# Seven products for eight in the w1/w3 pairs of the 512-token FFNs of a diffusion backbone in split fp32, with two weight sums added up by DMA, another memory layout and another place for the background adaLN work

## Chip, cores and metric

One NeuronCore of a Trainium2 chip runs the whole program in one launch. The metric is device time in microseconds (us), the median of several executions. The program is bound to one core, so nothing is exchanged with others.

## What is computed

Two layers over 512 tokens (256 latent tokens, 256 context tokens), D_MODEL 1024, D_FF 2816, all in float32. Each layer: half an FFN, a token mixer of three branches, half an FFN; each with an adaLN shift, scale and gate (nine vectors "mods" a layer, from `c @ w_ada`). The second layer's last FFN needs the 256 latent tokens only.

```python
def swiglu(h, w1, w3, w2):
    return (jax.nn.silu(h @ w1) * (h @ w3)) @ w2

x = x + 0.5 * m[:, 2] * swiglu(modulate(rms_norm(x, norm_g[l, 0]), m[:, 0], m[:, 1]),
                               ffn_w1[l, 0], ffn_w3[l, 0], ffn_w2[l, 0])
xc = xc + 0.5 * mc[2] * swiglu(modulate(rms_norm(xc, norm_g[l, 0]), mc[0], mc[1]),
                               ffn_w1[l, 0], ffn_w3[l, 0], ffn_w2[l, 0])
```

`x` are the latent tokens, `xc` the context tokens; both go through the same weights.

## The kernel before, in words

The stages are f00 (FFN), mixer 0, f01, f10 (FFNs of 512 tokens), mixer 1, f11 (FFN of 256 tokens) and the output. Activations lie channels on partitions, tokens along the row; a matmul multiplies a 128x128 block of weights with 512 (or 256) tokens.

fp32 accuracy comes from splitting each operand in a high and a low part of type fp32r: every block product is three matmuls, hi by hi, hi by lo and lo by hi (`mm3`, L280 to L282). Inputs are split once. Weights are split as they come: SP loads a tile of 512 KB (4 row blocks x 256 columns, `load_raw`) into one of four places `wr`, ScalarE (ACT) casts it to `whi` (L285), VectorE (DVE; for some tiles GpSimd, POOL) takes the difference as `wlo` (L286). Four pairs of places `wh` hold split weights, so the cast of the fifth waits for the last matmul of the first.

An FFN has 11 column pairs g; pair g is 256 columns of w1 (into PSUM tile p1) and the same 256 of w3 (p3). Each is 8 row blocks (two weight tiles) x 2 column blocks x 3 = 48 matmuls of 512 tokens, 96 for the pair (`product`). Then Silu (L607, ACT), the product with p3 (L608, DVE) and the split in `ghi` and `glo`. Pairs 0 to 5 are the first half, 6 to 10 the second; after each half `to_residual` multiplies with the rows of w2 that belong to it: four column groups of 256 columns, in chunks of up to four row blocks, and adds the result to the residual stream (`xT`, L507, four of 128x256 for each column group). In the second half the squares of the residual are summed for the next norm (`sq` on ACT, `acc_f` on DVE, L312), and the fourth column group is worked together with the next stage's first products (`handover`).

The adaLN vectors of later stages are computed beside the FFNs (`ada`, L200 to L224): a mod is eight steps, each loading 512 KB of w_ada and doing two passes of 128x1024 on DVE (`aacc`, L208, L210), and a ninth with a few small matmuls. `tick()` issues them evenly over the 56 products of an FFN: six mods in f00, five in f01, five in f10, none in mixers and f11.

The order of the instructions on each engine is made by a scheduler at build time; the engines then work through it in order and wait on semaphores. In the built program the hidden inputs `hhi`, `hlo` start at 43 and 59 KiB of each partition, the split weights lie from 91 to 123 KiB, `ghi` starts at 132 and `glo` at 156 KiB.

## Time and profile before

| | |
|---|---|
| median of 3 runs | 2013.01 us (2012.78 to 2013.74) |
| the profiled execution | 2012.76 us, its span 2011.0 us |
| mean granted clock of TensorE | 0.996 |
| busy | TensorE 1981.5 us, VectorE 1330.9, ScalarE 836.3, GpSimd 51.7 |
| matmuls | 11087 |
| read from HBM | 283.50 MB, 143 GB/s over the span |

The profile is of one execution. Busy times say what an engine did, the waits what it stood for, and the chain which work set the end. Matmuls overlap, so the distance from one start to the next, not the length of one, is what a matmul costs. The stages of the FFN f10 in the trace: first w1/w3 half to 1319.4 us, first w2 half to 1388.2, second w1/w3 half to 1500.5, second w2 half to 1547.

### The profile page before, as it was taken

The numbers are of one execution on the slowest core, as the hardware profiler recorded it, in microseconds if no ns is written. First come the engines' busy times: TensorE is split into PE (matmuls) and PEld (weight loads), VectorE is DVE, ScalarE is ACT, GpSimd is POOL, SyncE is SP. The second block draws the span as 40 slices with busy tenths as digits, with TensorE's granted clock in tenths as the row PEclk, the third lists the DMA queues.
The fourth block names the chain that finished last, engine by engine and source line by source line (L and its number), as shares of the span: only waits on it lengthen the run. The fifth ranks groups of instructions, "written<-read, shape, count | busy, mean of one in ns | idle before, by whom it ended". The sixth has DMA issues, their size and how long they took to land.

```text
span 2011.0 us, 27970 instructions
## 1 busy us (share of the span) xinstructions
PE 1981.5 (99%) x11087; PEld 1685.1 (84%) x11087; DVE 1330.9 (66%) x2038; ACT 836.3 (42%) x1286; POOL 51.7 (3%) x32
## 2 busy tenths in 40 slices
...
PEclk8999999999999999999999999999999999999999
...
GB/s 298 217 178 173 172 172 173 115 97 83 77 53 97 118 89 123 120 160 146 176 168 157 134 69 189 178 156 125 166 168 105 64 88 143 145 196 162 187 185 115
DMA packets 240507, 288.47 MB, mean 143 GB/s; under 512 B 14368, under 2 KB 222328, under 8 KB 240120
## 3 DMA queue, kind: packets, MB, share of 16 engines
q1 hardware_dynamic: 240376, 286.69, 46.3%
...
HBM read 283.50 MB, written 3.15 MB: 143 GB/s over the span
## 4 chain that ended last, share of the span: by engine, by line
PE 92%; DVE 3%; ACT 2%; DMA 2%; issue 1%; POOL 0%; SPq 0%; DVEq 0%; ACTq 0%; POOLq 0%
PE p L280 14%; PE p L281 14%; PE p L282 14%; PE py L280 8%; PE py L281 8%; PE py L282 8%; PE pg L282 3%; PE pg L281 3%; PE pg L280 3%; PE pj L281 2%; PE pj L280 2%; PE pj L282 2%; PE pv L809 1%; PE pv L810 1%; PE pv L811 1%; DMA wada<-w_ada 1%
## 5 line engine op out<-in xcount | busy, mean ns | idle before, releaser
L285 ACT CAST whi<-wraw 128x1024 fp32r<-128x1024 f32 (+2 forms) x408 | 406.4, 1000 | 943.6 <-PE p L281 417.0
L286 DVE TENSOR_TENSOR wlo<-wraw,whi 128x1024 fp32r<-128x1024 f32 (+2 forms) x380 | 445.0, 1177 | 348.4 <-ACT whi L285 347.4
L280 PE MATMUL p<-hhi_f,whi 128*128 128x512 f32 (+1 forms) x1440 | 516.1, 359 | 0.4 <-DVE hhi_f L352 0.4
L282 PE MATMUL p<-hhi_f,wlo 128*128 128x512 f32 (+1 forms) x1440 | 513.3, 356 | 1.1 <-POOL wlo L286 0.6
L281 PE MATMUL p<-hlo_f,whi 128*128 128x512 f32 (+1 forms) x1440 | 513.9, 357 | 0.2
L280 PEld LDWEIGHTS p<-hhi_f,whi 128*128 128x128 f32 x1440 | 272.3, 189 | 48.3 <-ACT whi L285 5.9
L282 PEld LDWEIGHTS p<-hhi_f,wlo 128*128 128x128 f32 x1440 | 272.3, 189 | 41.1 <-POOL wlo L286 1.3
L210 DVE SCALAR_TENSOR_TENSOR aacc<-wada,cs,aacc 128x1024 f32<-128x1024 f32 x224 | 277.3, 1279 | 42.6 <-DMA wada<-w_ada 42.3
L281 PEld LDWEIGHTS p<-hlo_f,whi 128*128 128x128 f32 x1440 | 272.3, 189 | 38.8 <-DVE hlo_f L357 1.0
L280 PE MATMUL py<-ghi,whi 128*128 128x512 f32 (+1 forms) x764 | 269.0, 352 | 0.0
L281 PE MATMUL py<-glo,whi 128*128 128x512 f32 (+1 forms) x764 | 267.6, 350 | 0.0
L282 PE MATMUL py<-ghi,wlo 128*128 128x512 f32 (+1 forms) x764 | 267.5, 350 | 0.0
L280 PEld LDWEIGHTS py<-ghi,whi 128*128 128x128 f32 x764 | 143.9, 188 | 26.1 <-issue 4.2
L282 PEld LDWEIGHTS py<-ghi,wlo 128*128 128x128 f32 x764 | 143.9, 188 | 21.3
L281 PEld LDWEIGHTS py<-glo,whi 128*128 128x128 f32 x764 | 143.9, 188 | 21.0
L280 PE MATMUL pg<-hhi_m,whi 128*128 128x512 f32 (+1 forms) x384 | 132.5, 345 | 0.0
L282 PE MATMUL pg<-hhi_m,wlo 128*128 128x512 f32 (+1 forms) x384 | 130.6, 340 | 1.3 <-DVE wlo L286 1.2
L281 PE MATMUL pg<-hlo_m,whi 128*128 128x512 f32 (+1 forms) x384 | 130.3, 339 | 0.0
L286 POOL TENSOR_TENSOR wlo<-wraw,whi 128x768 fp32r<-128x768 f32 (+2 forms) x28 | 51.5, 1842 | 1732.0 <-ACT whi L285 1675.0
L507 DVE SCALAR_TENSOR_TENSOR xT<-py,gmod,xT 128x256 f32<-128x256 f32 x136 | 59.1, 478 | 54.5 <-PE py L282 54.2
L280 PE MATMUL pj<-hhi_m,whi 128*128 128x256 f32 (+1 forms) x288 | 92.9, 323 | 0.0
L281 PE MATMUL pj<-hlo_m,whi 128*128 128x256 f32 (+1 forms) x288 | 92.7, 322 | 0.2
...
## 6 DMA issues: line engine op xcount, KB each, us to landing
wraw<-ffn_w SPq DMA_DIRECT2D x256, 512.0 KB, 3.8
wada<-w_ada SPq DMA_DIRECT2D x128, 512.0 KB, 3.8
wraw<-w_in SPq DMA_DIRECT2D x64, 512.0 KB, 3.6
...
wraw<-w_out SPq DMA_DIRECT2D x16, 512.0 KB, 3.4
...
```

The costliest lines, as they stand in the source:

```text
L210: v.scalar_tensor_tensor(acc[:, t], w, cs[:, k, t:t + 1], acc[:, t], op0=ALU.mult, op1=ALU.add)
L280: te.matmul(o, a, xh, start=start, stop=False)
L281: te.matmul(o, a, xl, start=False, stop=False)
L282: te.matmul(o, b, xh, start=False, stop=stop)
L285: s.copy(hi, src)
L286: eng.tensor_tensor(lo, src, hi.bitcast(F32), ALU.subtract)
L507: v.scalar_tensor_tensor(X[0][:, d, c], acc, gate[:, d, t:t + 1], X[0][:, d, c], op0=ALU.mult, op1=ALU.add)
L809: te.matmul(o, hhi[:, kk, ts], hi[:, k], start=(kk == 0), stop=False)
L810: te.matmul(o, hhi[:, kk, ts], lo[:, k], start=False, stop=False)
L811: te.matmul(o, hlo[:, kk, ts], hi[:, k], start=False, stop=(kk == KD - 1))
```

## The change

*Seven products.* For g = 3 to 10 in f00, f01 and f10 (24 pairs) the pair's work is seen as a product of a 2x2 matrix of weight blocks (w1 or w3; rows 0 to 511 or 512 to 1023) with a 2x2 matrix of input blocks (the same row halves; latent or context tokens), and done with seven block products in place of eight (`seven`, L636 to L683). In what follows P1 to P7 are these products in the order of the text: with w1's first row half (P1, bank b), w3's two halves added (P2, bank c), that sum and w1's first half (P3, b), w1's second half (P4, a tile of its own), w1's first and w3's first half (P5, b), a sum of four (P6, c), w3's second half (P7, b). Each is 4 row blocks x 2 column blocks x 3 = 24 matmuls (L655) of 256 tokens, 168 in all. Banks b and c are the two halves of one PSUM tile, and bank b goes on accumulating from P1 through P3 and P5 to P7. Between them what has been summed so far is read out: copies on ACT of q1 (L660, after P1), p5 (L663, after P2) and w1 (L667, after P3), additions on DVE (L670 after P4, L672 after P5, L676 after P6). In the built program each of P2, P3, P5, P6 and P7 waits for the readout before it, on whichever half of the tile that is. Two Silu (L679, L680) and two passes of DVE (L681, L683) make the gated result.

*Weight sums.* Of the four sums of weight tiles two are made by DMA: the first tile is loaded by SP, and GpSimd then issues a DMA that adds the second from HBM to it (L646, two a group, 48 in all). The other two are passes of DVE over 128x1024 (L665, L674), which the scheduler puts one group ahead of their use. A group splits seven tiles (before: four) and loads five by SP. `wr` has five places.

*Input forms.* `Forms` (L594) makes four sums of input blocks once an FFN, at g = 1 and 2: some twelve DVE passes of 128x1024 and the splits.

*Layout.* Split weights, `ghi` and `glo` of the 512-token FFNs lie below 128 KiB (from 42, 58, 74 and 98 KiB); hidden inputs and the input forms above (`hhi` 175, `hlo` 191, `zone0` 151, `zone1` 163). In f11 `ghi` and `glo` take the two zones.

*Background steps.* f00, f01 and f10 have four mods each, mixer 0 three (27 steps), f11 one. In the three FFNs five steps come at g = 2, the other 31 in the w2 stages, 1.55 for each chunk.

The diff, cut to what is spoken of:

```diff
--- before.py
+++ after.py
-    xp = ctx.enter_context(tc.tile_pool(name="xp", bufs=1))
-    hp = ctx.enter_context(tc.tile_pool(name="hp", bufs=1))
-    wr = ctx.enter_context(tc.tile_pool(name="wr", bufs=4))
+    sm = ctx.enter_context(tc.tile_pool(name="sm", bufs=2))
+    wr = ctx.enter_context(tc.tile_pool(name="wr", bufs=5))
     wh = ctx.enter_context(tc.tile_pool(name="wh", bufs=4))
-    sm = ctx.enter_context(tc.tile_pool(name="sm", bufs=2))
+
+    ctx.enter_context(tc.tile_pool(name="pad", bufs=1)).tile([P, 8], F32, name="pad")
+    xp = ctx.enter_context(tc.tile_pool(name="xp", bufs=1, side="right"))
+    hp = ctx.enter_context(tc.tile_pool(name="hp", bufs=1, side="right"))
+    tz = ctx.enter_context(tc.tile_pool(name="tz", bufs=1, side="right"))
+    sp = ctx.enter_context(tc.tile_pool(name="sp", bufs=1, side="right"))
+    hp.tile([P, 16], F32, name="pad")
...
+    def zone(i, dt=F32):
+        return tz.tile([P, 3 * D], dt, tag=f"t{i}", name=f"zone{i}")
+
+    def half_zone(i, dt=F32):
+        return sp.tile([P, 3 * NTOK], dt, tag=f"v{i}", name=f"half{i}")
+
+    def weight_places(n):
+
+        z = [zone(i, F32R).rearrange("p (a k n) -> p a k n", a=3, k=4) for i in range(2)]
+        if n == 2:
+            return [(z[0][:, 0], z[0][:, 1]), (z[1][:, 0], z[1][:, 1])]
+        return [(z[0][:, i], z[1][:, i]) for i in range(n)]
...
+    class Forms:
+
+
+        def __init__(self, norm, fp):
...
+            whole(t[0], h11, l11)
+            whole(t[1], h12, l12)
+            whole(t[2], h22, l22)
+            v.tensor_tensor(t[0], t[0], t[1], ALU.subtract)
+            v.tensor_tensor(t[1], t[2], t[1], ALU.subtract)
+            split_act(z[0][:, 0], z[1][:, 0], t[0])
+            split_act(z[0][:, 2], z[1][:, 2], t[1])
+            v.scalar_tensor_tensor(t[0], t[0], -1.0, t[2], op0=ALU.mult, op1=ALU.subtract)
+            whole(t[1], h21, l21)
+            split_act(z[0][:, 1], z[1][:, 1], t[0])
+            v.scalar_tensor_tensor(t[0], t[0], -1.0, t[1], op0=ALU.mult, op1=ALU.subtract)
+            self.fourth = lambda: split_act(h12, l12, t[0])
+            self.b11, self.b21, self.b22, self.t4 = (h11, l11), (h21, l21), (h22, l22), (h12, l12)
+            self.t1, self.t2, self.t3 = ((z[0][:, i], z[1][:, i]) for i in range(3))
...
+    def seven(fm, wa, wb, c0, gt):
+
+        q1, p5, w1 = fm.places()
+        pab, pc = psum("p1"), psum_bg("p3")
+        b, c, a = pab[:, 0], pab[:, 1], pc[:, 0]
+
+        def raw(w, i, *more):
+
+            t = load_raw([rowsof(w, 4 * i, 4, c0, 2 * P)], 4, 2 * P)
+            for w, i in more:
+                gp.dma_start(t, rowsof(w, 4 * i, 4, c0, 2 * P), accum_op=ALU.add)
+            return t
+
+        def part(o, w, x, first=False):
+            whi, wlo = split(w, 4, 2 * P)
+            for k in range(4):
+                for m in range(2):
+                    om, cm = o[:, m * L:(m + 1) * L], slice(m * P, (m + 1) * P)
+                    for n, (wt, xt) in enumerate(((whi, x[0]), (whi, x[1]), (wlo, x[0]))):
+                        te.matmul(om, wt[:, k, cm], xt[:, k], start=(first and k == m == n == 0),
+                                  stop=(k == 3 and m == 1 and n == 2), skip_group_check=True)
+
+        a11 = raw(wa, 0)
+        part(b, a11, fm.b11, True)
+        s.copy(q1, b)
+        s1 = raw(wb, 0, (wb, 1))
+        part(c, s1, fm.t1, True)
+        s.copy(p5, c)
+        s2 = fm.sum_place()
+        v.tensor_tensor(s2, s1, a11, ALU.add)
+        part(b, s2, fm.t2)
+        s.copy(w1, b)
+        a12 = raw(wa, 1)
+        part(a, a12, fm.b21, True)
+        v.tensor_tensor(q1, a, q1, ALU.add)
+        part(b, raw(wa, 0, (wb, 0)), fm.t3)
+        v.tensor_tensor(p5, b, p5, ALU.add)
+        s4 = fm.sum_place()
+        v.tensor_tensor(s4, s2, a12, ALU.add)
+        part(c, s4, fm.b22)
+        v.tensor_tensor(w1, c, w1, ALU.add)
+        g1, g2 = gt[:, :, 0:L], gt[:, :, L:]
+        q1, p5, w1, b3 = (x.rearrange("p (m n) -> p m n", m=2) for x in (q1, p5, w1, b))
+        s.activation(g1, q1, AF.Silu)
+        s.activation(g2, w1, AF.Silu)
+        v.scalar_tensor_tensor(g2, p5, -1.0, g2, op0=ALU.mult, op1=ALU.mult)
+        part(b, raw(wb, 1), fm.t4)
+        v.scalar_tensor_tensor(g1, b3, -1.0, g1, op0=ALU.mult, op1=ALU.mult)
...
+            rates = (1.25, (len(mods) * (KD + 1) - 5) / 20) if both else (0.8, 0.0)
+
+            def tick(rate):
+                due[0] += rate
+                n = int(due[0] + 1e-6)
+                due[0] -= n
                 with norm.done():
-                    background(want - state[1])
-                state[1] = max(want, state[1])
+                    background(n)
...
+                    if both and g > 2:
+                        seven(fm, w1, w3, g * 2 * P, gt)
+                        split_act(ghi[:, j, 0:nt], glo[:, j, 0:nt], gt)
+                        continue
...
+                            if g == 2 or not both:
+                                tick(rates[0])
...
+                    if both and g == 1:
+                        with norm.done():
+                            fm = Forms(norm, fp)
+                    if both and g == 2:
+                        fm.fourth()
+                for _ in to_residual(w2, nk, (ghi, glo), nt, gmod[l][:, f], st if half else None, fp, weights, 2 * g0,
                                      then):
-                    tick()
+                    tick(rates[1])
...
+            pending[:] = [ada(*m, mp) for m in mods]
+
+            def tick(n=1):
+                with entry.done():
+                    background(n)
...
+                    tick()
...
+                for n, _ in enumerate(merged(2, psum_bg, mm)):
+                    tick(n % 4 > 0)
...
+                for n, _ in enumerate(to_residual(I["w_out"][l], KD, (mhi, mlo), nq, gmod[l][:, 2], st, mm, weight_places,
+                                                  entry=then)):
+                    tick(2)
...
-    ffn(0, 0, NTOK, after, [(0, m) for m in range(2, 8)], entry)
+    ffn(0, 0, NTOK, after, [(0, m) for m in range(2, 6)], entry)
-    mixer(0, NTOK, entry, after)
+    mixer(0, NTOK, entry, [(0, m) for m in (6, 7, 8)], after)
-    ffn(0, 1, NTOK, after, [(0, 8)] + [(1, m) for m in range(4)], entry)
+    ffn(0, 1, NTOK, after, [(1, m) for m in range(4)], entry)
-    ffn(1, 0, NTOK, entry, [(1, m) for m in range(4, 9)], after)
+    ffn(1, 0, NTOK, entry, [(1, m) for m in range(4, 8)], after)
-    mixer(1, L, after, entry)
-    ffn(1, 1, L, entry, [], Output())
+    mixer(1, L, after, [], entry)
+    ffn(1, 1, L, entry, [(1, 8)], Output())
...
+    nc = _bacc.Bacc("TRN2", target_bir_lowering=False, num_devices=1, dynamic_dma_scratch_size=2048)
```

The order on ScalarE, at two groups of w1/w3. Before, in f10 (`whi` from `wraw` is a weight's cast, `gt` the Silu, L285 CAST `ghi` the split of the gated result):

```order
L285 CAST ghi<-gt 128x1024
L285 CAST whi<-wraw 128x1024 x2
L607 ACTIVATE gt<-p_9672 128x1024
L285 CAST whi<-wraw 128x1024 x2
L285 CAST ghi<-gt 128x1024
L285 CAST whi<-wraw 128x1024 x2
L607 ACTIVATE gt<-p_9811 128x1024
```

With the change, in f01, from the cast for P6 of one group to the cast for P5 of the next; the casts for P7, P1', P2', P3' and P4' (an apostrophe: the next group) are whi_9810, whi_9846, whi_9878, whi_9908 and whi_9939:

```order
L663 COPY half1_8017<-p1_9617 128x512
L306 CAST whi_9810<-wraw_9808 128x1024
L667 COPY w1_8018<-p1_9617 128x512
L306 CAST whi_9846<-wraw_9844 128x1024
L679 ACTIVATE gt_9616<-half0_8016 128x2x256
L306 CAST whi_9878<-wraw_9875 128x1024
L306 CAST whi_9908<-half1_8017 128x1024
L680 ACTIVATE gt_9616<-w1_8018 128x2x256
L306 CAST whi_9939<-wraw_9937 128x1024
L306 CAST ghi_9164<-gt_9616 128x1024
L660 COPY half0_8016<-p1_9842 128x512
L306 CAST whi_9971<-wraw_9968 128x1024
```

Where two casts stood between a Silu and a `ghi`, three copies out of PSUM now stand among seven casts; the cast for P7 comes ahead of the copy that P5 waits for, the cast for P4' and `ghi` ahead of the one that P2' waits for.

The order on TensorE, where one product ends and the next begins. Before, between w3 of one pair and w1 of the next (f10):

```order
L280 MATMUL p3_9961<-hhi_f10_9055,whi_10038 128x512
L281 MATMUL p3_9961<-hlo_f10_9056,whi_10038 128x512
L282 MATMUL p3_9961<-hhi_f10_9055,wlo_10039 128x512
L280 MATMUL p1_10099<-hhi_f10_9055,whi_10103 128x512
L281 MATMUL p1_10099<-hlo_f10_9056,whi_10103 128x512
L282 MATMUL p1_10099<-hhi_f10_9055,wlo_10104 128x512
```

With the change, in f01, behind P7: the last three of the eight matmuls of P1' that follow it, the first four of P4' (p3_9843), and the first of P2' (zone0, zone1 hold the input forms):

```order
L655 MATMUL p1_9842<-hhi_f01_7264,whi_9846 128x256
L655 MATMUL p1_9842<-hlo_f01_7265,whi_9846 128x256
L655 MATMUL p1_9842<-hhi_f01_7264,wlo_9847 128x256
L655 MATMUL p3_9843<-hhi_f01_7264,whi_9939 128x256
L655 MATMUL p3_9843<-hlo_f01_7265,whi_9939 128x256
L655 MATMUL p3_9843<-hhi_f01_7264,wlo_9940 128x256
L655 MATMUL p3_9843<-hhi_f01_7264,whi_9939 128x256
L655 MATMUL p1_9842<-zone0_7846,whi_9878 128x256
L655 MATMUL p1_9842<-zone1_7847,whi_9878 128x256
```

A product no longer runs from end to end. The whole order of a steady group is: 8 of P1', 4 of P4', all of P2', 13 of P4', all of P3', the last 7 of P4', all of P5', 8 of the next P1, all of P6', 8, all of P7', and the last 8.

The order on VectorE in the second w2 half, where the first and the second of its column groups end. Before, in f01:

```order
L507 SCALAR_TENSOR_TENSOR xT<-py,gmod_118,xT 128x256 x3
L217 COPY mrow<-pa_3_8823 128x512
L312 TENSOR_TENSOR acc_f_6865<-acc_f_6865,sq 128x256
L507 SCALAR_TENSOR_TENSOR xT<-py,gmod_118,xT 128x256
L220 TENSOR_TENSOR modT_114<-pa_3_8823,biasT_115 128x16
L286 TENSOR_TENSOR wlo<-wraw,whi 128x1024
L312 TENSOR_TENSOR acc_f_6865<-acc_f_6865,sq 128x256
L286 TENSOR_TENSOR wlo<-wraw,whi 128x1024 x3
L286 TENSOR_TENSOR wlo<-wraw,whi 128x512 x2
L507 SCALAR_TENSOR_TENSOR xT<-py,gmod_118,xT 128x256 x3
```

With the change, from the end of the first column group's residual; the `xT` of the second stand at L528 behind the eight `aacc`, and the `wlo` behind them is the third column group's first weight:

```order
L528 SCALAR_TENSOR_TENSOR xT<-py,gmod_124,xT 128x256
L233 SCALAR_TENSOR_TENSOR aacc<-wada,cs,aacc 128x1024
L333 TENSOR_TENSOR acc_f_7708<-acc_f_7708,sq 128x256
L233 SCALAR_TENSOR_TENSOR aacc<-wada,cs,aacc 128x1024 x7
L528 SCALAR_TENSOR_TENSOR xT<-py,gmod_124,xT 128x256 x3
L333 TENSOR_TENSOR acc_f_7708<-acc_f_7708,sq 128x256
L528 SCALAR_TENSOR_TENSOR xT<-py,gmod_124,xT 128x256
L333 TENSOR_TENSOR acc_f_7708<-acc_f_7708,sq 128x256
L307 TENSOR_TENSOR wlo<-wraw,whi 128x1024
L333 TENSOR_TENSOR acc_f_7708<-acc_f_7708,sq 128x256
L233 SCALAR_TENSOR_TENSOR aacc<-wada,cs,aacc 128x1024
L333 TENSOR_TENSOR acc_f_7708<-acc_f_7708,sq 128x256
```

Before, weights stood in a row ahead of the second column group's residual; now the background passes stand there, and the weight comes behind.

## Rows read from the trace of the kernel before

**Rows 1.** The page, part 1: busy us, share of the span, instructions, by engine

```profile
PE 1981.5 (99%) x11087; PEld 1685.1 (84%) x11087; DVE 1330.9 (66%) x2038; ACT 836.3 (42%) x1286; POOL 51.7 (3%) x32
```

**Rows 2.** The page, part 2: TensorE's granted clock in 40 slices of the span

```profile
PEclk8999999999999999999999999999999999999999
```

**Rows 3.** The page, part 4: the chain that ended last, by engine

```profile
PE 92%; DVE 3%; ACT 2%; DMA 2%; issue 1%; POOL 0%; SPq 0%; DVEq 0%; ACTq 0%; POOLq 0%
```

**Rows 4.** Waits: engine, line, releaser: us in total, times, longest us

```profile
ACT whi L285 <- PE p L281: 417.0, 133, 5.2
...
ACT whi L285 <- DMA wraw<-ffn_w: 112.0, 30, 9.4
```

**Rows 5.** Windows, f10's second w1/w3 half, mixer 0: PE, PEld, DVE, ACT, POOL, DMA

```profile
1388.20:1500.50 112.30, 112.30 (x506) 91.09 (x505) 72.08 (x69) 29.52 (x30) 0.00 (x0) 1.00 0.54 164
414.00:806.00 392.00, 388.78 (x1933) 315.69 (x1932) 261.33 (x496) 213.27 (x391) 20.81 (x12) 1.00 0.30 93
```

**Rows 6.** Timeline of PE, 512 columns: w1/w3 and w2 of f10 (start, us)

```profile
1404.25 0.39 PE L280 MATMUL p<-hhi_f,whi 128*128 128x512 f32 x1
...
1411.73 0.39 PE L280 MATMUL p<-hhi_f,whi 128*128 128x512 f32 x1
...
1349.74 0.40 PE L280 MATMUL py<-ghi,whi 128*128 128x512 f32 x1
...
1357.44 0.39 PE L280 MATMUL py<-ghi,whi 128*128 128x512 f32 x1
```

**Rows 7.** Timeline of PE, 256 columns: w1/w3 and w2 of f11

```profile
1919.85 0.28 PE L280 MATMUL p<-hhi_f,whi 128*128 128x256 f32 x1
...
1925.97 0.28 PE L280 MATMUL p<-hhi_f,whi 128*128 128x256 f32 x1
...
1978.99 0.28 PE L280 MATMUL py<-ghi,whi 128*128 128x256 f32 x1
...
1984.77 0.28 PE L280 MATMUL py<-ghi,whi 128*128 128x256 f32 x1
```

**Rows 8.** Lines by form, ACT: count, busy us, mean ns, idle before

```profile
L285 ACT CAST whi<-wraw 128x1024 fp32r<-128x1024 f32 x344 | 359.9, 1051 | 852.9 <-PE p L281 405.4 <-PE py L281 226.1 <-DMA wraw<-ffn_w 111.5
...
L985 ACT COPY aT<-pT 128x512 f32<-128x512 f32 x24 | 14.1, 587 | 12.2 <-PE pT L984 12.1
```

**Rows 9.** Lines by form, DVE

```profile
L286 DVE TENSOR_TENSOR wlo<-wraw,whi 128x1024 fp32r<-128x1024 f32 x340 | 413.9, 1221 | 299.8 <-ACT whi L285 298.9
...
L210 DVE SCALAR_TENSOR_TENSOR aacc<-wada,cs,aacc 128x1024 f32<-128x1024 f32 x224 | 277.3, 1279 | 42.6 <-DMA wada<-w_ada 42.3
...
L507 DVE SCALAR_TENSOR_TENSOR xT<-py,gmod,xT 128x256 f32<-128x256 f32 x136 | 59.1, 478 | 54.5 <-PE py L282 54.2
...
L1055 DVE SCALAR_TENSOR_TENSOR gt<-gt,pb 128x512 f32<-128x512 f32 x16 | 10.3, 683 | 14.3 <-PE pb L282 14.3
```

**Rows 10.** DMA issues: count, KB each, median us to landing

```profile
wraw<-ffn_w SPq DMA_DIRECT2D x256, 512.0 KB, 3.8
```

**Rows 11.** The page, part 3: queue, packets, MB, share of 16 engines

```profile
q1 hardware_dynamic: 240376, 286.69, 46.3%
```

**Rows 12.** Lines by form, PE: one of the three matmuls of each product

```profile
L280 PE MATMUL p<-hhi_f,whi 128*128 128x512 f32 x992 | 389.1, 392 | 0.0
...
L280 PE MATMUL py<-ghi,whi 128*128 128x512 f32 x468 | 185.8, 397 | 0.0
...
L280 PE MATMUL p<-hhi_f,whi 128*128 128x256 f32 x448 | 127.1, 284 | 0.4 <-DVE hhi_f L352 0.4
...
L280 PE MATMUL pg<-hhi_m,whi 128*128 128x512 f32 x192 | 76.5, 399 | 0.0
...
L280 PE MATMUL pg<-hhi_m,whi 128*128 128x256 f32 x192 | 56.0, 292 | 0.0
...
L280 PE MATMUL pj<-hhi_m,whi 128*128 128x256 f32 x192 | 55.0, 286 | 0.0
...
L280 PE MATMUL pj<-hhi_m,whi 128*128 128x512 f32 x96 | 37.9, 395 | 0.0
```

116 lines of the change are left out of this document (70 added, 46 removed).

## The prediction

> **What bounds the kernel now.** I read the page from the top. TensorE is busy 1981.5 of 2011.0 us [rows 1]; the granted clock is full in all slices after the first [rows 2]; the chain that ended last is 92% PE and the rest crumbs [rows 3]. So only two things can gain: less TensorE time, or the same with fewer gaps. VectorE (66%) and ScalarE (42%) have room on average. The waits say the same: ACT's cast of a weight waits for the matmul that last read its place, 417.0 us in 133 waits [rows 4]; weights wait for TensorE, not TensorE for weights. The window of f10's second w1/w3 half agrees: PE is busy from end to end [rows 5]. All sums are made against the profiled run, 2012.76 us with a span of 2011.0, that is 1.76 us around the span; the median is 2013.01. A difference under 0.2% (4 us) can't be told from none.
>
> What a matmul costs is read from start to start, since its own 0.39 us overlap the next. 512 columns: from 1404.25 to 1411.73 lie 33 steps, 0.2267 us each, where inputs and weights both lie below 128 KiB; in the w2 products, inputs above and weights below, 33 steps take 7.70 us, 0.2333 each [rows 6]. 256 columns: both below, 51 steps in 6.12 us, 0.1200; inputs above, 51 steps in 5.78 us, 0.1133 [rows 7]. So the trace has a price for either placement, though only in different stages.
>
> **The change, part by part.**
>
> *Seven products, 24 groups.* Before, a pair is 96 matmuls of 512 columns: 96 x 0.2267 = 21.76 us. Now it is 168 of 256 columns with inputs above and weights below: 168 x 0.1133 = 19.04 us. Products alone: -2.72 x 24 = -65 us. (At 0.1200 it would be 20.16 and -38.)
>
> *What that group adds on the handovers.* Before, each accumulator takes 48 matmuls and another tile is ready. Now banks b and c are one tile, and the program makes a product into one bank wait for the readout of the other: P2 for the copy of q1, P3 for p5's, P5 for w1's, P6 and P7 for the DVE adds before them. So nearly every product waits for a readout of the one before, and PE has only the pieces of P1' and P4 that its order puts between. ScalarE and VectorE work in order, and both orders put a weight split ahead of the readout. A cast takes 1.05 us, a copy of 128x512 out of PSUM 0.59 (the nearest row, aT), wlo 1.22, a 128x512 pass of DVE on PSUM 0.68 [rows 8, 9]. A cast can start when the last hi matmul of the product that used its place is done, one matmul (0.11) before the product's end.
>  - P3 to P5: ACT does the cast of w3's second chunk, then the copy of w1: 1.05 + 0.59 - 0.11 = 1.53 us. PE has 7 matmuls of P4 between: 0.79. Stall 0.74.
>  - P7 to P2': ACT does the cast of a12', then ghi, then the copy of q1: 1.05 + 1.05 + 0.59 - 0.11 = 2.58. PE has 8 + 4 matmuls, 1.36. Stall 1.22. Within it the fourth product's lo weight is late as well (0.94 + 1.22 = 2.16 against 1.13, its third matmul), which hides in the same gap.
>  - P2 to P3: 1.53 against 13 matmuls, 1.47: 0.06. P5 to P6, P6 to P7: 0.68 against 8 matmuls, 0.91: nothing, as long as DVE is free.
> Together 2.0 us a group: the period is 21.06, not 19.04. Over 24 groups the stalls are +48 us and the seven products are left with **-17 us**. Bounds: none of it, if ACT gets ahead of PE (0), and 2.6 with 0.1 us for each of six handovers (+62).
>
> *The accumulating DMAs.* The trace has none, nor any DMA from POOL. Loop: P5 ends, cast and split of s1' (1.05 + 1.22), its place is loaded again (3.8), added to (X), and then DVE's order has the sum s2'', wlo of t3', of s4', the sum s4'', the add at L670, wlo of w3_1' and of a11'' (6 x 1.22 + 0.68), which P1'' needs right behind P5'. So the period is at least 14.1 + X - 0.2, and X is hidden up to 7.2 us. The nearest row is the plain load of the same 512 KB, 3.8 us; two of them are 7.6; the longest wait of a cast for a load is 9.4 [rows 4, 10]. I take X between 3.8 and 7.2, nothing on the path, and keep 9.4: then the period is 23.3 and the cost (23.3 - 21.06) x 24 = +54 us. The Trainium skill (DMA: Bandwidth & Descriptors, on the anatomy of one SWDGE DMA) fits such a DMA as 2.0 us plus bytes by 436e3, an estimate of 3.2 us here, for a plain copy; by it X is hidden. No run here shows it. SDMA itself has room: 286.69 MB took 46.3% of the span, 1.70 us for 512 KB [rows 11]; seven in 21.06 us are 57%.
>
> *Placement elsewhere.* w2's 512 columns now have both operands below: 3 x 468 x 0.0066 = -9. 256-column products that turn from below to split (p, pg, pj: 3 x (448 + 192 + 192) = 2496) x 0.0067 = -17. 512-column products whose inputs go above (pg and pj 3 x 288, and g 0 to 2 of three FFNs, 3 x 992 less 24 x 96 = 672) x 0.0066 = +10 [rows 12]. **-16 us** together; the ends are 0 (the placement was not the cause of the steps) and -26.
>
> *The moved ada steps.* They leave the w1/w3 stages, where DVE had room (72 of 112 us [rows 5]), for the w2 stages, at 1.55 steps of 2 x 1.28 us per chunk of 5.4 us. In the second w2 half DVE's order now has eight aacc behind the first column group, and the wlo of the third group's first chunk only behind four xT and two acc_f of the second (before, the wlo stood ahead). PE runs into it: 4 x 0.48 + 2 x 0.48 (an acc_f priced as an xT of its size) + 1.22 - 0.45 (two hi matmuls) = 3.6 us; then two acc_f, four aacc and a wlo, 7.3 us, against 5.4 of matmuls, some 1.5 more [rows 9]. 5 us in each of three FFNs: **+15**. Below: 0, if the order's DVE runs ahead. In the first w2 half DVE has 3 x 1.22 + 14 x 1.28 at most + 4 x 0.48 a column group against 72 x 0.2267 = 16.3, full but not yet late: **+3** for three. In mixer 0, 27 steps add 27 x 2 x 1.28 = 69 us to 261 of 392 [rows 5]; covered but for a few readouts that queue behind one: **+4** with f11's nine steps. Cover gone, each would cost its 1.28.
>
> *Forms.* Some twelve DVE passes of 1.22 us fall at g = 1 and 2 and stand ahead of weights: one and a half passes' lateness, **+4.5** for three FFNs.
>
> Sum: -17 - 16 + 15 + 3 + 4 + 4.5 = -6.5 on 2012.76: **2006 us**.
>
> **Rivals.**
>  1. *The handovers are covered.* ScalarE runs ahead of its order, since most casts have their weights early; half the stalls (24) and of the DVE bunching (12) go: 2006 - 24 - 12 = 1970. For it: ACT busy 42%. Against: the cast of each late place waits for PE by its place, however free ACT is.
>  2. *The accumulating DMA is late* (slower). X over 7.2 us puts (X - 7.2) x 24 on top; from X = 7.6 the gain is gone, at 8 it is over 0.2% slower, at 9.4 it is 2006 + 54 = 2060. For it: two hops in a row, a read of the destination, a queue that the trace never shows. Against: 3.8 for the same bytes.
>  3. *Placement gives nothing*, the steps of 0.1133 and 0.2333 belong to the stage and its inputs: then seven products run at 0.1200 (+27) and the 16 us are gone: 2006 + 43 = 2049. For it: each pair of steps was read in two different stages. Against: the four steps are steady. The Trainium skill (TensorE: Matmul & The Clock Gate, on the back-to-back issue gap) has N/2.4 + 2.5 ns, 215.8 and 109.2, whatever the place; the rows differ from it by 4 to 18 ns and by place. By that formula alone the sum would be 24 x (20.72 - 18.34) = 57 for the products and nothing for placement: 2006 + 8 + 16 = 2030.
>  4. The change does less than it says: no; the order shows 24 such groups.
>
> **How the numbers follow.** Forecast 0.42 (1990 to 2022 by the bounds of its small terms: of these 0.28 faster, 0.08 same, 0.06 slower), rival 1 0.20 (faster), rival 2 0.26 (0.04 same, 0.22 slower), rival 3 0.12 (0.02 same, 0.10 slower). Faster 0.48, same 0.14, slower 0.38. The range goes from a little below rival 1 to a little above rival 2 at 9.4, 1958 to 2065; beyond lie X over 9.6 and a full cover of every handover.
>
> **What would show it.** In a w1/w3 half PE starts in steps of 0.113 us, in a group of about 21 us, with gaps of 0.7 before L655's fifth product and 1.2 before the second, released by ACT L667 and L660; PE's busy share there falls to about 90%. The accumulating DMA lands in under 7 us. PE has a gap of some 3 us in each second w2 half, released by a DVE wlo. Wrong would be: a group under 19.5 us (rival 1), DVE's sums waiting on the accumulating DMA (rival 2), steps of 0.120 (rival 3).

## The result, and the profile after

The changed kernel takes 2165.97 us (four runs, 2163.69 to 2173.61) against 2013.1: ratio 1.0766, 95% interval 1.0739 to 1.0792. It is 153 us slower, where 7 us faster was forecast, and lies 101 us above the stated range. The profiled execution has a span of 2161.9 us.

The page after, busy times by engine, the granted clock in 40 slices, the DMA queues and the chain; they answer to [rows 1], [rows 2], [rows 11] and [rows 3]:

```profile
PE 2009.9 (93%) x12815; PEld 1763.5 (82%) x12815; DVE 1561.3 (72%) x2290; ACT 956.0 (44%) x1466; POOL 116.3 (5%) x80
PEclk8999999999999999999999999999899999999999
q1 hardware_dynamic: 253048, 299.27, 44.6%
q0 software_dynamic: 25344, 25.17, 7.9%
PE 65%; DMA 11%; DVE 11%; issue 7%; ACT 4%; POOL 0%; SPq 0%; DVEq 0%; POOLq 0%; ACTq 0%
```

TensorE's share of the span fell from 99 to 93%, its share of the chain from 92 to 65%. DMA and DVE stand in the chain with 11% each where they had 2 and 3. TensorE, which waited for almost nothing before, now waits for the others.

The stages, from the first matmul of each in the trace (us). In the changed kernel the last two products, P6 and P7, of each half's last group run behind the first matmuls of w2, some 6 us of work that the table counts to the w2 stage:

| stage | before | after |
|---|---|---|
| w1/w3, first half: f00, f01, f10 | 142.0, 134.9, 134.3 | 150.1, 143.9, 139.4 |
| w2, first half: f00, f01, f10 | 68.8, 68.8, 68.8 | 76.2, 76.2, 76.3 |
| w1/w3, second half: f00, f01, f10 | 112.3, 112.2, 112.3 | 125.3, 130.7, 125.8 |
| second w2 half of f00 and mixer 0 | 461.1 | 489.2 |
| second w2 half of f01 | 58.5 | 70.9 |
| second w2 half of f10 and mixer 1 | 312.5 | 324.6 |
| f11 to the end | 198.0 | 206.9 |

No stage got shorter. Two pictures of one second half, that of f01, show what a group looks like. First a steady group, from one copy of q1 to the next (timeline of ScalarE: start, length):

```profile
1125.92 0.58 ACT L660 COPY half<-p 128x512 f32<-128x512 f32 x1
1148.66 0.58 ACT L660 COPY half<-p 128x512 f32<-128x512 f32 x1
```

and TensorE's gaps in it and at its two ends (timeline of TensorE; in brackets the idle time and what ended it):

```profile
1126.38 0.39 PE L655 MATMUL p<-hhi_f,wlo 128*128 128x256 f32 x1 [0.76 <-DVE wlo L307]
1135.89 0.52 PE L655 MATMUL p<-zone,whi 128*128 128x256 f32 x2 [0.72 <-ACT w L667]
1149.12 0.39 PE L655 MATMUL p<-hhi_f,wlo 128*128 128x256 f32 x1 [0.75 <-DVE wlo L307]
```

The group takes 22.74 us. One of the two stops that were predicted is there: P5 waits for the copy of w1. The other is not ahead of P2' but a few matmuls earlier, at the third matmul of P4', which waits for its lo weight. Measured as the step from one start to the next less an ordinary one, each is 0.9 us.

Then the start of the same run of groups, where the w2 stage ends at 1087.3 us (timeline of TensorE):

```profile
1089.99 0.28 PE L655 MATMUL p<-hhi_f,wlo 128*128 128x256 f32 x1
1094.57 0.58 PE L655 MATMUL p<-hhi_f,whi 128*128 128x256 f32 x1 [4.30 <-ACT whi L306]
1094.94 0.41 PE L655 MATMUL p<-hlo_f,whi 128*128 128x256 f32 x1
1101.13 0.79 PE L655 MATMUL p<-zone,whi 128*128 128x256 f32 x2 [5.77 <-ACT half L660]
```

TensorE does P1, stands 4.3 us for a cast, does two matmuls of P4 and stands 5.8 us for the copy of q1. What ScalarE did meanwhile, and GpSimd's DMAs (timelines of both):

```profile
1091.26 1.04 ACT L306 CAST whi<-wraw 128x1024 fp32r<-128x1024 f32 x1 [10.98 <-DMA wraw<-ffn_w]
1092.52 1.04 ACT L306 CAST whi<-half 128x1024 fp32r<-128x1024 f32 x1 [0.21 <-DVE half L665]
1093.47 1.04 ACT L306 CAST whi<-wraw 128x1024 fp32r<-128x1024 f32 x1
1099.55 1.04 ACT L306 CAST whi<-wraw 128x1024 fp32r<-128x1024 f32 x1 [5.04 <-DMA wraw<-ffn_w]
1100.50 0.58 ACT L660 COPY half<-p 128x512 f32<-128x512 f32 x1
```

```profile
1082.33 1.29 POOL L646 DMA_DIRECT2D wraw<-ffn_w  x1 [98.71 <-DMA wraw<-ffn_w]
1091.48 1.30 POOL L646 DMA_DIRECT2D wraw<-ffn_w  x1 [7.86 <-issue]
```

ScalarE has its casts and copies in one order. The cast of s1 waits till 1091.26 for the tile that the DMA issued at 1082.33 adds; the cast for P4, whose weight needs no sum, stands behind it. Then the cast of t3 waits till 1099.55 for the DMA issued at 1091.48, and the copy of q1, whose product P1 had ended by 1090.3, stands behind that one. And the clock follows (windows of 4 us: length, busy of PE, PEld, DVE, ACT, POOL, granted clock, DMA share, GB/s):

```profile
1088.00:1092.00 4.00, 2.27 (x20) 2.06 (x18) 0.81 (x1) 0.74 (x1) 0.52 (x1) 1.00 0.37 116
1096.00:1100.00 4.00, 0.00 (x0) 0.00 (x0) 1.40 (x2) 0.45 (x1) 0.00 (x0) 0.50 1.13 285
1100.00:1104.00 4.00, 2.87 (x13) 2.87 (x14) 2.36 (x2) 1.08 (x2) 1.29 (x1) 0.50 0.31 55
```

With TensorE standing, the granted clock fell to 0.50, which is 1.2 of 2.4 GHz, and stayed there while it worked again: the matmuls from 1101.5 to 1104.3 come in steps of 0.21 us, the later ones in 0.118 again.

The two other second halves start in the same way (two stops, 9 us together). The three first halves start with one stop of 6.9 to 8.9 us, which comes through VectorE: its sum s2 waits for the added tile, and the lo weight that TensorE needs stands behind it (f01; timelines of VectorE, then TensorE):

```profile
944.43 1.22 DVE L665 TENSOR_TENSOR half<-wraw 128x1024 f32<-128x1024 f32 x1 [9.24 <-DMA wraw<-ffn_w]
947.98 0.58 PE L655 MATMUL p<-hhi_f,wlo 128*128 128x256 f32 x1 [8.62 <-DVE wlo L307]
```

That is the sign that the prediction had set for its rival 2. Over the whole trace this is who stood idle till an accumulating DMA had landed (instructions of L646, who waited for them: us in total, times):

```profile
  DVE half L665: 77.2, 20
  ACT whi L306: 64.7, 9
```

How long the accumulating DMAs take, beside the plain loads (DMA issues: count, KB each, median us to landing), answers to [rows 10]:

```profile
wraw<-ffn_w SPq DMA_DIRECT2D x280, 512.0 KB, 4.5
...
wraw<-ffn_w POOLq DMA_DIRECT2D x48, 512.0 KB, 7.1
```

7.1 us, from 5.9 to 10.8, and issuing one takes GpSimd 1.3 us. The Trainium skill (DMA: Bandwidth & Descriptors, on the anatomy of one SWDGE DMA) gives 2.0 us plus bytes by 436e3, 3.2 us as an estimate, for a plain copy on this path; the trace disagrees for one that adds, by more than twice. The added bytes also hold the DMA engines longer: by the queues above 25.17 MB took 7.9% of the 16 engines' span, 3.6 us for 512 KB, the plain loads (299.27 MB in 44.6%) 1.7 us.

### The profile page after: what moved, and what is told of

It reads as the page before. It is cut to its first block, busy times and chain, and to the rows that moved or that the text cites. A ratio compares the mean times of both kernels' runs of the same rounds, so it can differ in the third digit from the quotient of the medians.

```text
span 2161.9 us, 32134 instructions
## 1 busy us (share of the span) xinstructions
PE 2009.9 (93%) x12815; PEld 1763.5 (82%) x12815; DVE 1561.3 (72%) x2290; ACT 956.0 (44%) x1466; POOL 116.3 (5%) x80
## 3 DMA queue, kind: packets, MB, share of 16 engines
q1 hardware_dynamic: 253048, 299.27, 44.6%
q0 software_dynamic: 25344, 25.17, 7.9%
## 4 chain that ended last, share of the span: by engine, by line
PE 65%; DMA 11%; DVE 11%; issue 7%; ACT 4%; POOL 0%; SPq 0%; DVEq 0%; POOLq 0%; ACTq 0%
PE p L655 12%; DMA wraw<-ffn_w 7%; PE py L301 7%; PE py L303 7%; PE py L302 7%; DVE wlo L307 4%; PE p L302 3%; PE p L303 3%; PE p L301 3%; DMA wada<-w_ada 3%; PE pg L303 3%; PE pg L302 3%; PE pg L301 3%; DVE aacc L233 2%; ACT whi L306 2%
## 5 line engine op out<-in xcount | busy, mean ns | idle before, releaser
L655 PE MATMUL p<-zone,whi 128*128 128x256 f32 x1152 | 222.9, 294 | 43.0 <-ACT half L660 31.1
L655 PE MATMUL p<-hhi_f,wlo 128*128 128x256 f32 x768 | 218.9, 290 | 41.9 <-DVE wlo L307 41.9
L655 PE MATMUL p<-hhi_f,whi 128*128 128x256 f32 x768 | 224.6, 297 | 15.7 <-ACT whi L306 13.5
L655 PEld LDWEIGHTS p<-zone,whi 128*128 128x128 f32 x1152 | 184.5, 197 | 58.5 <-ACT half L660 33.2
L303 PE MATMUL p<-hhi_f,wlo 128*128 128x256 f32 (+1 forms) x672 | 216.0, 322 | 5.3 <-DVE wlo L307 4.7
L655 PE MATMUL p<-hlo_f,whi 128*128 128x256 f32 x768 | 219.4, 287 | 0.0
L301 PE MATMUL p<-hhi_f,whi 128*128 128x256 f32 (+1 forms) x672 | 216.9, 323 | 0.4 <-DVE hhi_f L373 0.4
L302 PE MATMUL p<-hlo_f,whi 128*128 128x256 f32 (+1 forms) x672 | 216.2, 322 | 0.3
L303 PE MATMUL py<-ghi,wlo 128*128 128x512 f32 x468 | 187.0, 400 | 9.3 <-DVE wlo L307 9.3
L301 PE MATMUL py<-ghi,whi 128*128 128x512 f32 x468 | 188.6, 403 | 0.0
L302 PE MATMUL py<-glo,whi 128*128 128x512 f32 x468 | 187.0, 400 | 0.0
L655 PEld LDWEIGHTS p<-hhi_f,wlo 128*128 128x128 f32 x768 | 148.2, 194 | 46.0 <-DVE wlo L307 46.0
L655 PEld LDWEIGHTS p<-hhi_f,whi 128*128 128x128 f32 x768 | 149.9, 195 | 25.2 <-ACT whi L306 20.3
L655 PE MATMUL p<-zone,wlo 128*128 128x256 f32 x576 | 165.7, 288 | 0.9 <-DVE wlo L307 0.9
L655 PEld LDWEIGHTS p<-hlo_f,whi 128*128 128x128 f32 x768 | 149.8, 195 | 0.4
```

The source lines that it names most:

```text
L301: te.matmul(o, a, xh, start=start, stop=False)
L302: te.matmul(o, a, xl, start=False, stop=False)
L303: te.matmul(o, b, xh, start=False, stop=stop)
L655: te.matmul(om, wt[:, k, cm], xt[:, k], start=(first and k == m == n == 0), stop=(k == 3 and m == 1 and n == 2), skip_group_check=True)
```

## The experiments

| kernel | us | ratio to before, 95% interval |
|---|---|---|
| before | 2013 | 1 |
| 1: layout alone | 2034.5 | 1.0091 to 1.0121 |
| 2: layout and moved adaLN steps | 2065.5 | 1.0245 to 1.0275 |
| 3: changed, no added tile | 2076.1 | 1.0298 to 1.0329 |
| 4: changed, same bytes copied away, nobody waits | 2080.4 | 1.0314 to 1.0348 |
| the change | 2166.0 | 1.0739 to 1.0792 |
| 5: changed, bank c beside a | 2138.6 | 1.0564 to 1.0647 |
| 6: changed, weights moved by 32 bytes | 2159.7 | 1.0709 to 1.0741 |
| 7: sums from four loaded tiles | 2131.0 | 1.0565 to 1.0601 |
| 8: 7 and bank c beside a | 2069.3 | 1.0263 to 1.0305 |
| 9: 8 and aligned operands | 2040.8 | 1.0118 to 1.0149 |
| 10: 9 and adaLN steps spread | 2017.5 | 1.0011 to 1.0029 |
| 11: 10 and one split on GpSimd | 2035.9 | 1.0101 to 1.0131 |
| 12: before, aligned operands | 2002.9 | 0.9934 to 0.9961 |

The theory from the trace was that the added tile, not TensorE's work, sets the ends; the rivals were DMA traffic, the handovers between products, the layout and the moved steps. Each kernel is built anew, so that its edit also moves what the scheduler orders around it.

**1, layout alone.** Seven products and forms out, adaLN steps back in their places:

```diff
-                    if both and g > 2:
+                    if False:
...
-    ffn(0, 0, NTOK, after, [(0, m) for m in range(2, 6)], entry)
+    ffn(0, 0, NTOK, after, [(0, m) for m in range(2, 8)], entry)
...
-    mixer(0, NTOK, entry, [(0, m) for m in (6, 7, 8)], after)
+    mixer(0, NTOK, entry, [], after)
```

> The changed kernel with its seven products and input forms taken out (all pairs as 96 matmuls of 512 columns) and the adaLN steps put back where they were; memory layout and the fifth weight place stay. Compared with the kernel before (2013). Placement as predicted (operands below 128 KiB 0.2267, split 0.2333 for 512 columns; split 0.1133 for 256): w2 gains 9, small products gain 17, 2976 + 864 matmuls of 512 columns lose 0.0066 each, 25: about 2012. Rival, what the changed kernel's trace shows (0.2333 for all 512 columns, 0.118 for all 256): 25 lost on 512 columns, w2 unchanged, 256 columns about even: about 2038, and no gap in the second w2 halves.

Measured 2034.5, 21 us slower than before: the rival. By the prediction's prices this kernel would have taken about what the one before takes; the layout costs 21 us.

**2, layout and moved steps.** As 1, with the lists and rates of the changed kernel.

> The changed kernel without seven products and forms, but with its layout and its places for the adaLN steps. Against the layout alone this is the price of the moved steps. As predicted: 15 + 3 + 4 = 22 us over it. By the stage table of the changed kernel (w2 halves, mixers and f11 together some 60 us longer, less what layout costs there): 40 to 55 us over it. The gap of 3 us in each second w2 half must be there.

Measured 2065.5, 31 us over layout alone, between what was predicted (22) and what the stage table suggested. The gap in the second w2 half is there (timeline of TensorE, f01):

```profile
1187.89 0.40 PE L302 MATMUL py<-glo,whi 128*128 128x512 f32 x1
1191.22 0.50 PE L303 MATMUL py<-ghi,wlo 128*128 128x512 f32 x1 [2.94 <-DVE wlo L307]
```

One of about 3 us stands in each of the three FFNs, where 3.6 was worked out from the order.

**3, no added tile.**

```diff
-                gp.dma_start(t, rowsof(w, 4 * i, 4, c0, 2 * P), accum_op=ALU.add)
+                pass
```

> The changed kernel without its 48 accumulating DMAs: the two weight sums are just their first tile, so the gated results are wrong in value; everything else runs. If the accumulating DMA sets the stops of 10 us at the start of each run of groups (its 7.1 us come behind a base load that itself starts late), each of six starts loses about 7 us of stop and some of the low clock that follows: 50 to 60 us faster than the changed kernel, with the steady group still at 22.8. If loads alone set those stops: under 15 us.

Measured 2076.1: 90 us faster than the changed kernel, more than expected. The same second half of f01 in one window, first without and then with the added tile (columns as in the windows above):

```profile
1048.30:1156.80 108.50, 100.52 (x795) 95.52 (x794) 78.22 (x78) 50.66 (x62) 0.00 (x0) 1.00 0.44 129
```

```profile
1087.30:1218.00 130.70, 106.27 (x796) 100.22 (x795) 79.70 (x80) 51.68 (x63) 11.67 (x9) 0.93 0.62 148
```

It is 108.5 for 130.7 us, with the clock at 1.00 for 0.93. The groups are 22.7 to 22.8 us from the first to the last, where the changed kernel has 25.4, 22.7, 27.7 and 27.8 in this half. So the steady group does not owe its length to the accumulating DMAs, but the stops at the starts and in the longer groups come from them.

**4, the same bytes.** The accumulating DMA is replaced by one that copies the loaded tile away to HBM.

```diff
-                gp.dma_start(t, rowsof(w, 4 * i, 4, c0, 2 * P), accum_op=ALU.add)
+                gp.dma_start(dram.tile([P, 4, 2 * P], F32, name=f"away{next(away)}"), t)
```

> The changed kernel with each accumulating DMA replaced by a DMA of the same 512 KB, issued by GpSimd at the same place and behind the same load, that copies the loaded tile to HBM: the sums are left out (the first tile alone is used), GpSimd and the DMA engines work as before, but no cast and no sum waits for it. If what cost 90 us is the wait for the added tile (7.1 us in a chain with load, sum and split): about the time without sums, 2076 to 2090, groups of 22.8. If it is the traffic or GpSimd's queue: over 2130.

Measured 2080.4, 4 us over kernel 3: that GpSimd issues 48 more DMAs and 25 MB more move costs next to nothing. But the work of GpSimd and of the DMA engines is not the same as with adding, which the expectation had taken it to be (DMA queues, answering to the line of q0 above):

```profile
q0 software_dynamic: 6912, 25.17, 3.0%
```

The copies take 6912 packets and 3.0% of the engines' span where the adding DMAs took 25344 and 7.9%, and issuing one takes GpSimd 0.53 us where it took 1.3. So kernel 4 clears the bytes, not the longer time on the engines. That the sums, casts and copies stand and wait for the added tile is in the trace above; that the same time on the engines, with nobody waiting, would be free is not shown.

**5, bank c beside a.**

```diff
-        b, c, a = pab[:, 0], pab[:, 1], pc[:, 0]
+        b, c, a = pab[:, 0], pc[:, 1], pc[:, 0]
```

> The changed kernel with banks b and c in different PSUM tiles (c beside a in the third tile), so that a product waits only for readouts of its own tile. If the shared tile makes the handovers, the steady group falls from 22.8 by most of the 2.2 us of its gaps, to 20.8 to 21.5: 30 to 45 us faster in all. If the order on ScalarE makes them (P5 needs the copy of its own bank, P4' its own weight), the gaps of 0.9 stay and the group stays above 22.3: under 12 us.

Measured 2138.6, 27 us faster, just short of the first case. The shortest groups fall to 19.8 to 21.6 us, and the one from 1114.9 us on (20.4 us) has no stop at all in TensorE's timeline; others rise to 23 to 30: with shorter groups the chain through the added tile comes to the fore. Kernels 7 and 8 differ by the same line without accumulating DMAs: there it is worth 62 us, 2131.0 to 2069.3. The shared tile made the handovers, and their price depends on what else is late.

**6, weights moved by 32 bytes.** In the kernel before and after, the step of a matmul did not go by the half of SBUF: the changed kernel's w2 has both operands below 128 KiB and still takes 0.2333 us (27 steps from 1470.06 to 1476.36).

```diff
-    ctx.enter_context(tc.tile_pool(name="pad", bufs=1)).tile([P, 8], F32, name="pad")
...
     sm = ctx.enter_context(tc.tile_pool(name="sm", bufs=2))
+    ctx.enter_context(tc.tile_pool(name="pad", bufs=1)).tile([P, 8], F32, name="pad")
     wr = ctx.enter_context(tc.tile_pool(name="wr", bufs=5))
```

> The changed kernel with one pad of 32 bytes moved from behind the split weights to ahead of them, so that only their addresses change, from 0 to 32 modulo 128 (hidden inputs 96, input forms 32, ghi and glo 32, as in the changed kernel). If what counts is the distance of the two operands modulo 128 bytes (in the kernel before: 0 for w1/w3, 64 for w2): products with hidden inputs (distance 64) run at 0.1133, those with forms (0) at 0.120, w2 (0) at 0.2267; 9 us from w2, 11 from the small products, 5 from the seven: about 2141. If the half of SBUF or the stage counts: no step changes, 2166.

Measured 2159.7, 6 us faster where 25 was expected, but the steps came as the distance says. First the changed kernel (w2 of f10, then w1/w3 of f11, 60 steps), then kernel 6 (w2 of f01, 30 steps, and w1/w3 of f11, 51 steps; timelines of TensorE):

```profile
1470.06 0.39 PE L301 MATMUL py<-ghi,whi 128*128 128x512 f32 x1
...
1476.36 0.40 PE L301 MATMUL py<-ghi,whi 128*128 128x512 f32 x1
...
2071.89 0.28 PE L301 MATMUL p<-hhi_f,whi 128*128 128x256 f32 x1
...
2078.99 0.28 PE L301 MATMUL p<-hhi_f,whi 128*128 128x256 f32 x1
```

```profile
1028.06 0.39 PE L301 MATMUL py<-ghi,whi 128*128 128x512 f32 x1
...
1034.86 0.39 PE L301 MATMUL py<-ghi,whi 128*128 128x512 f32 x1
...
2074.97 0.28 PE L301 MATMUL p<-hhi_f,whi 128*128 128x256 f32 x1
...
2080.75 0.28 PE L301 MATMUL p<-hhi_f,whi 128*128 128x256 f32 x1
```

w2 went from 0.2333 to 0.2267 and f11 from 0.1183 to 0.1133 when nothing but the weights' address moved by 32 bytes, with all tiles in the same halves. By the stages, the first w2 halves got 1.8 to 1.9 us shorter each and f11 3.2; the w1/w3 halves, where TensorE waits, came out between 1.1 us shorter and 4.9 longer. Why some got longer is open.

**7, sums from four loaded tiles.** s1 and t3 by GpSimd, s2 and s4 by VectorE; the tile for P7 is kept from the first load:

```diff
-        s1 = raw(wb, 0, (wb, 1))
+        b11, b12 = raw(wb, 0), raw(wb, 1)
+        s1 = fm.sum_place()
+        gp.tensor_tensor(s1, b11, b12, ALU.add)
...
+        gp.tensor_tensor(b11, b11, a11, ALU.add)
...
-        part(b, raw(wa, 0, (wb, 0)), fm.t3)
+        part(b, b11, fm.t3)
...
-        v.tensor_tensor(s4, s2, a12, ALU.add)
+        v.tensor_tensor(a12, s2, a12, ALU.add)
...
-        part(b, raw(wb, 1), fm.t4)
+        part(b, b12, fm.t4)
```

> The changed kernel with all four weight sums made from the four tiles once loaded (two sums by GpSimd, two by VectorE): four loads a group for five loads and two accumulating DMAs. If the accumulating DMA and the reloading set the stops at the start of each run of groups: close to the kernel without sums, 2070 to 2085, the steady group still near 22.8. If the held tiles or GpSimd's slow sums (2.6 us each) stop the next group: over 2110.

Measured 2131.0, the second case. In the second halves the first three groups take about 27 us each, the others 22.7 to 26. VectorE's sum waits for GpSimd's, and all that is behind it in its order with it (timelines of GpSimd, then VectorE and TensorE, in one group):

```profile
1109.81 2.38 POOL L663 TENSOR_TENSOR half<-wraw 128x1024 f32<-128x1024 f32 x1 [20.41 <-DMA wraw<-ffn_w]
1112.27 3.44 POOL L668 TENSOR_TENSOR wraw<-wraw 128x1024 f32<-128x1024 f32 x1
```

```profile
1112.22 1.23 DVE L667 TENSOR_TENSOR half<-half,wraw 128x1024 f32<-128x1024 f32 x1 [4.32 <-POOL half L663]
1113.36 0.68 DVE L673 TENSOR_TENSOR half<-p,half 128x512 f32<-128x512 f32 x1
1113.96 3.96 DVE L307 TENSOR_TENSOR wlo<-wraw,whi 128x1024 fp32r<-128x1024 f32 x2
1117.97 0.39 PE L655 MATMUL p<-hhi_f,wlo 128*128 128x256 f32 x1 [2.81 <-DVE wlo L307]
```

The two wlo beside GpSimd's sum take 3.96 us, where two alone take 2.4: they end at 1117.92, 2.2 us after GpSimd's sum (1115.71), as if they had not moved while it ran. GpSimd's second sum, which began while VectorE's ran, took 3.44 us where the first took 2.38. TensorE then stands 2.8 us for the wlo.

**8, 7 with bank c beside a.** The line of kernel 5.

> The same with bank c beside a instead of beside b. If the two causes add up (stops from the accumulating DMA, handovers from the shared tile): the group near 20.5 to 21 in a row, 2025 to 2045. If ScalarE's and VectorE's order takes the place of the shared tile: 2060 or more.

Measured 2069.3, the second case. The shortest groups are 21.1 to 21.4 us, the first and the last of a second half 23.5 to 25. The stop that is left most often is ahead of P6 (timeline of TensorE, then its waits: us in total, times, longest us):

```profile
1085.31 0.39 PE L655 MATMUL p<-hhi_f,whi 128*128 128x256 f32 x1 [0.80 <-DVE half L673]
PE p L655 <- DVE half L673: 30.8, 18, 4.0
```

L673 is the addition on VectorE that reads P4 out. Bank c now shares its tile with a, P4's bank, so that P6 waits for that readout, which comes late in VectorE's order. So one shared tile was given up for another, and VectorE's order sets its price.

**9, 8 with aligned operands.** The pad of kernel 6, and the 64 bytes behind the hidden inputs taken out, so that the input forms lie at 96 and the weights at 32 modulo 128.

```diff
-    hp.tile([P, 16], F32, name="pad")
```

> The same with split weights at 32 and input forms at 96 modulo 128, so that every 256-column product has the distance 64 and w2 the distance 0. If the distance counts: all 256 columns at 0.1133 (4032 in the seven, 2496 elsewhere, 0.0045 each, 29 us) and w2 at 0.2267 (9 us): 25 to 40 us faster than the one before it here. If not: the same as that one.

Measured 2040.8, 28.5 us faster than kernel 8, as expected of the distance.

**10, adaLN steps spread.**

```diff
-            rates = (1.25, (len(mods) * (KD + 1) - 5) / 20) if both else (0.8, 0.0)
+            rates = (1.25, (len(mods) * (KD + 1) - 17) / 20) if both else (0.8, 0.0)
...
                         split_act(ghi[:, j, 0:nt], glo[:, j, 0:nt], gt)
+                        tick(1.5)
                         continue
```

> The kernel with sums from four tiles, bank c beside a and aligned operands (2041), with 12 of the 31 adaLN steps of each 512-token FFN moved out of the w2 stages into the eight groups of seven products, 1.5 a group. If VectorE's bunches in the w2 stages are the rest of the loss (the moved steps cost 31 alone): 10 to 20 us faster, the gap in the second w2 halves gone. If VectorE has no room left in a group of 21 us: the groups get longer by what is put in, 3 to 4 us each, and it is slower by 40 or more.

Measured 2017.5, 23 us faster than kernel 9: the bunches were the loss. The gaps in the second w2 halves of the three FFNs are gone, and these halves are 7 to 8 us shorter each. VectorE had room for the moved steps, but not for nothing: the middle groups of the second halves, 21.0 us in kernel 9, take 22.3 to 23.0, while the first and the last got 0.4 to 1.1 us shorter. Still 1.002 of the kernel before. By the stages, the second w2 half of f00 with mixer 0, which keeps its 27 steps, is 14.6 us longer than before; all the rest together is 9 us shorter.

**11, one split on GpSimd.**

```diff
-        part(b, b12, fm.t4)
+        part(b, b12, fm.t4, eng=gp)
```

> The same with the lo split of the seventh product's weight on GpSimd (2.6 us there for 1.2 on VectorE). If VectorE's order sets the gap of 1.2 us before P6 (its add at the readout of P4 comes late): 20 us faster than the one before it here. If GpSimd's split comes too late for P7: slower than it by up to 24 x 1.4.

Measured 2035.9, 18 us slower than kernel 10, as in the second case, but not by its mechanism: TensorE doesn't wait for P7's lo weight. The stop ahead of P6 got longer (TensorE's waits, kernel 10, then 11: us in total, times, longest us; then VectorE's timeline in kernel 11):

```profile
PE p L654 <- DVE half L672: 20.5, 12, 4.3
PE p L654 <- DVE half L672: 37.7, 12, 6.4
1047.27 3.34 DVE L666 TENSOR_TENSOR half<-half,wraw 128x1024 f32<-128x1024 f32 x1 [5.90 <-POOL half L662]
```

L672 is the addition that reads P4 out. It stands behind VectorE's sum L666, which waits for GpSimd's sum and then, beside GpSimd's split (1047.19 to 1049.53), takes 3.34 us for 1.2. So VectorE's order does set the gap before P6, and GpSimd, to which the split was given, is what VectorE waits for.

**12, the kernel before, aligned.** Views shifted by 64 bytes:

```diff
-            self.hi = hp.tile([P, KD, NTOK], F32R, tag="hhi", name=f"hhi_{self.name}")
-            self.lo = hp.tile([P, KD, NTOK], F32R, tag="hlo", name=f"hlo_{self.name}")
+            n, o = KD * NTOK, 16 * (self.nt == NTOK)
+            h = hp.tile([P, 2 * n + 16], F32R, tag="hh", name=f"hh_{self.name}")
+            self.hi, self.lo = (h[:, o + i * n:o + (i + 1) * n].rearrange("p (k n) -> p k n", k=KD) for i in range(2))
...
-                ghi = fp.tile([P, 12, NTOK], F32R, tag="ghi", name="ghi")
-                glo = fp.tile([P, 12, NTOK], F32R, tag="glo", name="glo")
+                n, o = 12 * NTOK, 16 * (nt == NTOK)
+                ghi = fp.tile([P, n + 16], F32R, tag="ghi", name="ghi")[:, o:o + n].rearrange("p (k n) -> p k n", k=12)
+                glo = fp.tile([P, n + 16], F32R, tag="glo", name="glo")[:, 16 - o:16 - o + n].rearrange("p (k n) -> p k n", k=12)
```

> The kernel before with views shifted by 64 bytes and nothing else: hidden inputs, ghi and glo of the 512-token stages at distance 0 modulo 128 from the weights, those of f11 at distance 64. If the distance sets the steps: 1404 matmuls of w2 at 0.2267 for 0.2333 (9 us) and 1344 of f11 at 0.1133 for 0.120 (9 us), nothing else changed: 1992 to 1998. If the half of SBUF or the stage sets them: 2013.

Measured 2002.9, ratio 0.9948 (0.9934 to 0.9961): the only kernel here that is faster than the kernel before. It is some 8 us short of what was expected. w2, with ghi above and weights below 128 KiB as before, now runs at 0.2267 (30 steps), but f11's 256 columns, both operands below, at 0.1179 (57 steps), not at 0.1133 (timeline of TensorE, f10's w2, then f11's w1/w3):

```profile
1339.64 0.39 PE L280 MATMUL py<-ghi,whi 128*128 128x512 f32 x1
...
1346.44 0.39 PE L280 MATMUL py<-ghi,whi 128*128 128x512 f32 x1
...
1911.06 0.28 PE L280 MATMUL p<-hh_f,whi 128*128 128x256 f32 x1
...
1917.78 0.28 PE L280 MATMUL p<-hh_f,whi 128*128 128x256 f32 x1
```

## Why the prediction was wrong

The kernels 1, 2 and 3 split the 153 us into four steps, taken in this order. Kernel 1 still has the 24 pairs as matmuls of 512 columns, with inputs above 128 KiB; by the prediction's price that costs 24 x 96 x 0.0066 = 15 us, which seven products then take away again. So its -16 for placement is -1 here, and its -12.5 for seven products and forms is -28:

| step | by the prediction's prices | measured | from |
|---|---|---|---|
| layout alone | -1 | +21 | kernel 1 less before |
| moved adaLN steps | +22 | +31 | kernel 2 less kernel 1 |
| seven products and forms, no added tile | -28 | +10.5 | kernel 3 less kernel 2 |
| accumulating DMAs | 0 | +90 | the change less kernel 3 |

The last step is the largest. But without it the kernel would still take 2076, 11 us above the stated range, so the placement and the seven products were wrong as well.

**The accumulating DMAs (the step that failed).** The prediction said: "I take X between 3.8 and 7.2, nothing on the path". X is 7.1, inside that interval, and for the steady group the loop holds: 14.1 + 7.1 - 0.2 = 21.0 is under 22.7. What failed is the premise of a steady state. The loop hides X behind the group before; at six starts there is no such group, ScalarE's order holds a cast and a copy that need no sum behind casts that do, and a run is only three to five groups long. At the start of a second half X comes twice in a row and TensorE stands for 9 to 10 us, at the start of a first half once, for 7 to 9, and the clock falls to half. Rival 2 named the mechanism, with its price worked out for steady groups (54 us at 9.4), so that it was too cheap, and it had a chance of 0.26. The two traces also show how the loss divides. Counted from start to start over the matmuls of the seven products, TensorE's stops add up to 113 us with the added tile and 45 without; 53 us of the 113 are at the six starts, 24 in nine stops of over 2 us in later groups. The matmuls at the clock of 0.50 take 21 us longer than at full clock, against none. So some 68 us are standing and some 21 the low clock. That the bytes are not the cause kernel 4 shows; what part the longer time on the DMA engines has in X, and so in the 90 us, stays open.

**Placement.** The prediction took the steps of [rows 6, 7] for an effect of the two halves of SBUF, from two stages that differed in more than that. Its rival 3 was right in that the halves are not the cause, but neither is the stage or its inputs, as it had it, and its 0.1200 and 2049 did not come: what counts is the distance of the two operands modulo 128 bytes. At 512 columns the changed layout brought every product from 0.2267 to 0.2333 or left it there; in kernel 1 that is some 3840 matmuls by 0.0066, 25 us. At 256 columns it gives 0.118, not 0.1133, so that the 2496 small matmuls gain 4 us, not 17. Together that is the 21 us of kernel 1. Kernels 6 and 9 show the distance by moving addresses alone; kernel 12 does so for w2, and only in part for f11.

**Seven products.** Handovers of 2.0 us a group were predicted, with stops of 0.74 for P5 and 1.22 ahead of P2'. Measured are 0.9 for P5, 0.9 on the lo weight of P4' and small ones of 0.2 to 0.3 us, 2.2 together. The sum came out, but the second stop stands at the wait that the prediction had said would hide. What was mis-sized is the step: with 0.118 for 0.1133 (168 x 0.118 = 19.8) and some 0.7 us for steps that are longer right behind a wait, that makes the 22.7 of the trace; 21.06 was predicted. So a group of seven products is longer than the 21.76 of the 96 matmuls it replaces, which is a loss at any price of the sums; in kernel 9, with banks and addresses set otherwise, it is 21.0.

**Moved steps.** The mechanism was right and the gap in each second w2 half (3.6 predicted, about 3 us) as well; the sum, 22 for 31, is nearer than its terms, which is luck. By the stages of kernel 2 against kernel 1, the w2 halves, mixer 0 and f11 got 46 us longer: 1.6 in each first w2 half, about 7 in each second one (5 were predicted), some 11 in mixer 0 and 8.1 in f11, where the prediction had 4 for both. (For the first w2 halves its own sum, 3 x 1.22 + 14 x 1.28 + 4 x 0.48 = 23.5 us of VectorE against 16.3, is not "full but not yet late"; the 3 us set for them were a guess that came near the 5 measured.) Against that the w1/w3 halves, which the steps left, got 16 us shorter, a gain that the prediction did not count. So the cover of an engine that is busy for two thirds was not a cover in mixer 0; which of its readouts queued is not shown. Kernel 10 got 23 us back by spreading the steps.
